# Second feed-forward network: 18 of 22 pairs of up tiles computed as seven products of blocks instead of eight

## The chip, the core and the metric

The kernel runs on one core of one Trainium2 chip. The metric is the device time of one execution, in microseconds (us). The engines that matter are TensorE (PE in the profile, with its weight loads as PEld), VectorE (DVE), ScalarE (ACT) and the DMA queue that SyncE issues (SPq). Each engine takes its instructions in its own order and waits for others by semaphores.

## The reference

A two-layer network steps 512 latent and 128 context tokens of width 1024. Layer 0 mixes tokens with a state-space scan, layer 1 with attention; behind each stands a gated feed-forward network with a convolution of width 3 over the tokens:

```
def conv_ffn(h, up_w, conv_w, conv_b, down_w):
    u = dwconv(h @ up_w, conv_w, conv_b)
    a, v = jnp.split(u, 2, axis=-1)
    return (jax.nn.silu(a) * v) @ down_w
```

`up_w` is 1024 x 5632, `down_w` 2816 x 1024, all in float32. The residual sum, gated, and a last norm follow. The other outputs (scan states, keys, values) are not touched by the change.

## The kernel before

**Layout.** All activations lie transposed: 8 feature tiles of 128 partitions by T = 640 tokens. A float32 operand is kept as a pair: a high part, rounded to the format that TensorE multiplies (`hi`, by ScalarE), and the rest (`lo = x - hi`, by VectorE). A product of two such operands is three matmuls: hi x hi, hi x lo, lo x hi.

**Weights** come in units of up to 128 x 1024 floats (512 KB). `prefetch` (L119) issues a unit's DMA into one of four `raw` buffers; `cast` (L127) splits it on ScalarE (`whi`, L95) and VectorE (`wlo`, L101); `nextw` (L140) keeps the loads three units and the split one unit ahead of TensorE.

**A feed-forward network** (`ffn`, L538) has 22 hidden tiles p (FT). Each needs a *pair* of up tiles: an `a` tile and a `v` tile of 128 features. `next_tile` (L314) runs `dense` over all 8 feature tiles of h: 8 steps x 3 matmuls, each cut into 256 and 384 columns (the halves A and B of the tokens) because a PSUM bank ends there; 48 matmuls a tile, 96 a pair. `copy_out` (L544) brings a tile from PSUM to SBUF on ScalarE. `epilogue` (L550) then does, for both tiles, the convolution (`conv`, L530: one ScalarE instruction and four on VectorE, of 511 and 127 columns), SiLU, the product and the split of the result into `mh` and `ml`, which are the moving operands of the down projection.

**Order.** `SUB` cuts the 22 hidden tiles into three groups, (0,8), (8,15) and (15,22). A stage of up pairs runs up to one pair past its group; then a down stage adds that group's share to all 8 output tiles (`project_out`, L275; for the last group `project_last`, L283, which also feeds the last norm). So the second network is: up 9 pairs, down 8 hidden tiles, up 7 pairs, down 7, up 6 pairs, down 7. Its first three up tiles come from `start_tiles` (L305), interleaved with the norm of h. The order in which each engine's instructions stand is fixed when the program is built: Python emits them in program order, and a scheduler of the framework may move them within an engine where dependencies allow.

**Places.** PSUM has three double banks (`dense_ps`, L115) for up and down tiles. The split weights have five buffers in the feed-forward networks (three in `pw`, two in `px`). Between the stages ScalarE and VectorE have much less to do than within the up stages.

Of the kernel before, what the change touches and what calls it, by code (L numbers as in the profile page):

```python
# [18 lines left out]
P = 128  # L19
D = 1024  # L20
KT = D // P
TP = 128
TS = 512
T = TP + TS
# [18 lines left out]
RSQRT_MAGIC = float(0x5F3759DF)  # L43


class Step:


    def __init__(self, ctx, tc, a):
        self.ctx, self.tc, self.nc, self.a = ctx, tc, tc.nc, a  # L50
        self.tasks = []
        self.ticks = 0
        self.wi = 0
        self.normt = {}
        self.ready = []
        self.px = None
        self.modtask = None
        self.late = []
        self.down = False
        self.wraw, self.wcast = {}, {}  # L60
        self.units = []
        pool = lambda n, b, **k: ctx.enter_context(tc.tile_pool(name=n, bufs=b, **k))
# [37 lines left out]
    def tt(self, out, a, b, op):  # L100
        return self.nc.vector.tensor_tensor(out, a, b, op)  # L101

    def mm(self, out, lhsT, rhs, start, stop):
        return self.nc.tensor.matmul(out, lhsT, rhs, start=start, stop=stop)  # L104

    def ct(self, shape, name, dt=F32):
        return self.pc.tile(shape, dt, tag=name, name=name)
# [11 lines left out]
    def prefetch(self, upto):  # L119
        while len(self.wraw) <= min(upto, len(self.units) - 1):  # L120
            u = len(self.wraw)
            ap, n = self.units[u]
            r = self.pw.tile([P, 1024], F32, tag="raw", name=f"raw{u}", bufs=RAW)
            self.nc.sync.dma_start(r[:, :n], ap)
            self.wraw[u] = r

    def cast(self, upto):  # L127
        while len(self.wcast) <= min(upto, len(self.units) - 1):
            u = len(self.wcast)
            self.prefetch(u)  # L130
            n = self.units[u][1]
            r = self.wraw[u]
            wp, t, b = (self.pw, "w", 3) if self.px is None or u % 5 < 3 else (self.px, "x", 2)
            hi = wp.tile([P, 1024], F32R, tag=t + "hi", name=f"whi{u}", bufs=b)
            lo = wp.tile([P, 1024], F32R, tag=t + "lo", name=f"wlo{u}", bufs=b)
            self.act(hi[:, :n], r[:, :n], AF.Copy)
            self.tt(lo[:, :n], r[:, :n], hi[:, :n].bitcast(F32), ALU.subtract)
            self.wcast[u] = (hi, lo)

    def nextw(self):  # L140
        u = self.wi
# [24 lines left out]
    def rsqrt(self, y, ms, n, count):  # L166
# [108 lines left out]
    def project_out(self, h, ks, g, tiles=range(KT)):  # L275

        for i in tiles:
            ps = self.dense_ps("po")
            self.dense(ps, self.nextw(), ks, h)
            for hf in "AB":  # L280
                self.gate_add(i, ps, g, hf)

    def project_last(self, h, ks, g, nextnorm, ks_last=None, parts="AB"):  # L283


        self.norm_begin()
        for i in range(KT - 3):
            ps = self.dense_ps("po")
            self.dense(ps, self.nextw(), ks, h)
            for hf in "AB":  # L290
                self.gate_add(i, ps, g, hf)
                self.norm_sq(i, hf)
        ks = ks_last or ks
        if self.modtask:
            self.drain(self.modtask)
        ws = [(self.dense_ps("po"), self.nextw(), i) for i in range(KT - 3, KT)]
        for hf in parts:
            for grp in ((ws[0:1], ws[1:3]) if hf == "B" else (ws[0:1], ws[1:2], ws[2:3])):
                self.dense_many([(ps, w, P) for ps, w, i in grp], ks, h, hf)
                for ps, w, i in grp:  # L300
                    self.gate_add(i, ps, g, hf)
                    self.norm_sq(i, hf)
            self.normt[hf] = self.add(nextnorm(hf), 3)
# [192 lines left out]
    def mod_rest(self, l, t0, pool):  # L496
# [41 lines left out]
    def ffn(self, l, h, nextnorm, pool):  # L538
        nc = self.nc
        cw = pool.tile([P, 2 * FT, 4], F32, tag="fcw", name=f"fcw{l}", bufs=1)  # L540
        nc.sync.dma_start(cw, self.a["fcw"][l])
        mid = {}

        def copy_out(ps):  # L544

            u = self.slot("f", "uraw", bufs=NF)
            self.act(u, ps[:, PO:PO + T], AF.Copy)
            return u

        def epilogue(p, ua, uv):  # L550
            ca = self.tmp("ca")
            self.conv(ca, ua, cw[:, p, :])
            cv = self.tmp("cv")
            self.conv(cv, uv, cw[:, FT + p, :])
            self.act(ca, ca, AF.Silu)
            self.tt(cv, ca, cv, ALU.mult)
            hi = self.slot("mh", f"mh{p}", F32R, bufs=9, pool=pool)
            lo = self.slot("ml", f"ml{p}", F32R, bufs=9, pool=pool)
# [10 lines left out]
        for s, (k0, k1) in enumerate(SUB):  # L569
            self.down = False  # L570
            while done < min(k1 + 1, FT):
                pair(done)
                done += 1
            self.down = True
            if s == len(SUB) - 1 and self.modtask:
                self.drain(self.modtask)
            if s < len(SUB) - 1:
                self.project_out(mid, range(k0, k1), self.gate(l, 1))
            else:
                self.project_last(mid, range(k0, k1), self.gate(l, 1), nextnorm, parts="CD" if l else "AB")  # L580


    def ssd_consts(self, pool):
# [505 lines left out]
    def attention(self, h, nextnorm, pool):  # L1089
# [5 lines left out]
        for hd in range(8):  # L1095
# [35 lines left out]
    def weight_units(self):  # L1131
        a = self.a
        u = [(a["w_dt"], 512)]
        xbc = lambda g: [16 + 4 * g + t for t in range(4)] + [32 + g, 36 + g]
        z = lambda g: [4 * g + t for t in range(4)]
        order = xbc(0) + xbc(1) + z(0) + xbc(2) + z(1) + xbc(3) + z(2) + z(3)
        u += [(a["w_in"][j], 1024) for j in order]
        for hf in range(2):
            u += [(a["w_so"][i, :, hf * 1024:(hf + 1) * 1024], 1024) for i in range(KT)]

        def ffn(l):
            done = 0
            out = []
            for k0, k1 in SUB:
                while done < min(k1 + 1, FT):
                    out.extend([(a["w_up"][l, done], 1024), (a["w_up"][l, FT + done], 1024)])
# [12 lines left out]
        return u  # L1159
# [131 lines left out]
```

## Time and profile before

| | us |
|---|---|
| median of three runs | 1894.25 |
| lowest and highest run | 1893.16, 1895.83 |
| span of the profiled execution | 1888.7 |
| PE, DVE, ACT busy in the span | 1855.0, 1366.3, 952.8 |

The profiled execution has no time of its own beside its span; the span runs from its first to its last instruction, and the median of the runs lies 5.5 us above it. The page's "busy" of an instruction runs from its start to its listed end, and successive instructions of one engine may overlap, so a sum of listed durations can exceed the busy time. In the rows of the timeline, the first two columns are the start and the length, both in us, and an x4 merges four instructions. In the chain of work that ended last, a row is a stretch in which one engine and one line carried the chain.

The second network lies at the end of the span. Its up and down stages can be read from the chain's rows `up` (up tiles) and `po` (down tiles).

### The profile page before, as it was taken

What the parts mean: (1) busy time and instruction counts of PE and PEld (TensorE: products, weight loads), DVE (VectorE), ACT (ScalarE), POOL (GpSimd) and SP (SyncE); (2) the same over time, 40 slices, a digit from 0 to 9 for tenths busy, and PEclk for the clock granted to TensorE, in tenths of its full rate; (3) what the DMA queues carried; (4) which work ended last, traced back from release to release, by engine and by line L of the source; (5) the groups of instructions that cost most, each with busy time, mean ns of one, the idle gap of its engine ahead of it and who ended that gap; (6) DMA issues with size and microseconds to landing.
All of it is one profiled execution on the core that took longest, in us unless ns stands there. A gap on an engine that the chain in (4) does not pass through costs nothing.

```text
span 1888.7 us, 32898 instructions
## 1 busy us (share of the span) xinstructions
PE 1855.0 (98%) x13333; PEld 1751.6 (93%) x13333; DVE 1366.3 (72%) x2640; ACT 952.8 (50%) x1748; POOL 0.2 (0%) x4
## 2 busy tenths in 40 slices
PE   7999999999999999999999999999999999999997
PEld 4799999989999999999999988888899999999996
DVE  4689999999758999974455877788686543553554
ACT  3479687878336441442443656566446432441441
POOL 0000000000000000000000000000000000000000
PEclk9999999999999999999999999999999999999998
DMA  9734243436533557632222211111132222222211
GB/s 346 261 108 139 97 145 107 133 123 197 186 107 124 189 173 227 190 102 80 75 70 71 74 57 57 60 48 38 36 124 79 79 74 73 74 72 79 73 40 56
DMA packets 79519, 209.71 MB, mean 111 GB/s; under 512 B 9116, under 2 KB 15880, under 8 KB 79240
## 3 DMA queue, kind: packets, MB, share of 16 engines
q1 hardware_dynamic: 78792, 207.10, 34.5%
q8 instruction: 104, 1.70, 0.4%
q10 hardware_dynamic: 576, 0.52, 0.1%
q14 instruction: 47, 0.39, 0.1%
HBM read 201.63 MB, written 5.96 MB: 110 GB/s over the span
## 4 chain that ended last, share of the span: by engine, by line
PE 93%; DVE 2%; ACT 2%; DMA 1%; issue 1%; SPq 0%; DVEq 0%; ACTq 0%
PE up L104 31%; PE po L104 25%; PE z L104 6%; PE x L104 5%; PE st L104 5%; PE v L104 3%; PE yp L104 3%; PE bc L104 2%; PE q L104 2%; PE sl L104 2%; PE k L104 2%; PE ov L104 2%; PE in L104 1%; PE wt L1065 1%; PE modrow L104 1%; ACT e L95 1%
## 5 line engine op out<-in xcount | busy, mean ns | idle before, releaser
L95 ACT ACTIVATE whi<-raw 128x1024 fp32r<-128x1024 f32 (+4 forms) x230 | 234.9, 1022 | 381.0 <-PE po L104 240.2
L101 DVE TENSOR_TENSOR wlo<-raw,whi 128x1024 fp32r<-128x1024 f32 (+4 forms) x230 | 270.2, 1175 | 176.2 <-ACT whi L95 164.7
L98 DVE SCALAR_TENSOR_TENSOR xr<-po,mod,xr 128x256 f32<-128x256 f32 (+2 forms) x231 | 88.8, 433 | 158.8 <-PE po L104 158.6
L104 PE MATMUL po<-mh,whi 128*128 128x256 f32 (+1 forms) x704 | 167.7, 310 | 0.0
L104 PE MATMUL po<-ml,whi 128*128 128x256 f32 (+1 forms) x704 | 167.5, 310 | 0.0
L104 PE MATMUL po<-mh,wlo 128*128 128x256 f32 (+1 forms) x704 | 167.3, 309 | 0.0
L104 PE MATMUL up<-h11h,wlo 128*128 128x256 f32 (+1 forms) x656 | 149.4, 309 | 0.0
L104 PE MATMUL up<-h01h,wlo 128*128 128x256 f32 (+1 forms) x656 | 149.4, 309 | 0.0
L104 PE MATMUL up<-h01l,whi 128*128 128x256 f32 (+1 forms) x656 | 149.3, 309 | 0.0
L104 PE MATMUL up<-h11h,whi 128*128 128x256 f32 (+1 forms) x656 | 149.3, 308 | 0.0
L104 PE MATMUL up<-h11l,whi 128*128 128x256 f32 (+1 forms) x656 | 149.3, 308 | 0.0
L104 PE MATMUL up<-h01h,whi 128*128 128x256 f32 (+1 forms) x656 | 149.3, 308 | 0.0
L104 PEld LDWEIGHTS po<-mh,whi 128*128 128x128 f32 x704 | 128.5, 188 | 0.6 <-ACT mh L95 0.4
L104 PEld LDWEIGHTS po<-mh,wlo 128*128 128x128 f32 x704 | 128.7, 188 | 0.0
L104 PEld LDWEIGHTS po<-ml,whi 128*128 128x128 f32 x704 | 128.6, 188 | 0.0
L104 PEld LDWEIGHTS up<-h01h,wlo 128*128 128x128 f32 x656 | 119.3, 188 | 0.0
L104 PEld LDWEIGHTS up<-h11h,whi 128*128 128x128 f32 x656 | 119.3, 188 | 0.0
L104 PEld LDWEIGHTS up<-h11h,wlo 128*128 128x128 f32 x656 | 119.3, 188 | 0.0
L104 PEld LDWEIGHTS up<-h11l,whi 128*128 128x128 f32 x656 | 119.3, 188 | 0.0
L104 PEld LDWEIGHTS up<-h01l,whi 128*128 128x128 f32 x656 | 119.3, 188 | 0.0
L104 PEld LDWEIGHTS up<-h01h,whi 128*128 128x128 f32 x656 | 119.3, 188 | 0.0
L95 ACT ACTIVATE mh<-cv 128x640 fp32r<-128x640 f32 x44 | 32.4, 737 | 121.3 <-DVE cv L101 121.3
(498 smaller groups left out, 4426.2 us busy)
## 6 DMA issues: line engine op xcount, KB each, us to landing
raw<-in_w_up SPq DMA_DIRECT2D x88, 512.0 KB, 3.5
mw<-in_modT SPq DMA_DIRECT2D x48, 512.0 KB, 4.3
raw<-in_w_in SPq DMA_DIRECT2D x40, 512.0 KB, 5.3
rb<-rowd SPq DMA_DIRECT2D x40, 512.0 KB, 5.3
raw<-in_w_dn SPq DMA_DIRECT2D x32, 448.0 KB, 3.3
raw<-in_w_qkv SPq DMA_DIRECT2D x24, 512.0 KB, 3.5
mr<-in_mod SPq DMA_DIRECT2D x44, 256.0 KB, 5.6
raw<-in_w_so SPq DMA_DIRECT2D x16, 512.0 KB, 4.2
```

The lines of the kernel that those rows point to most:

```text
L95: return self.nc.scalar.activation(out, in_, func, **k)
L98: return self.nc.vector.scalar_tensor_tensor(out, in0, s, in1, op0, op1)
L101: return self.nc.vector.tensor_tensor(out, a, b, op)
L104: return self.nc.tensor.matmul(out, lhsT, rhs, start=start, stop=stop)
L1065: nc.tensor.transpose(pm[:, b * P:(b + 1) * P], ws[b][:, kc * P:(kc + 1) * P], self.ident)
```

## The change

In the second network (l = 1), pairs 4 to 21 are no longer computed tile by tile. A pair is taken as a 2 x 2 block product: rows are the a tile and the v tile, the inner dimension is halved (feature tiles 0 to 3 and 4 to 7), and the columns are two halves of 320 tokens. The Winograd form of Strassen's scheme computes it with seven block products in place of eight.

- **Sums of h**, once: T1, T2, T4 (each for j = 0..3, 320 columns, split in hi and lo) and T3, which is written over a half of h that pairs 4 to 21 don't read any more. They are made during pairs 1 to 3 (`sums`, a task that moves on three `hook` steps at a time) and after pair 3 (`finish_sums`).
- **Sums of weights**, for each pair: s1 = y1+y2, s2 = s1-x1, s3 = x1-y1, s4 = x2-s2, where x and y are the raw a and v units and 1, 2 their halves of 512 columns; all on VectorE, in float32. Seven left operands of 512 columns (x1, x2, s2, s1, s3, s4, y2) are then split, against four halves (two whole units) before. The five split buffers hold two operands each. Splits run `LOOK` = 7 products ahead.
- **Products**: each is 4 steps x 3 matmuls of 320 columns; a pair is 84 matmuls. Four of the seven add onto another product in PSUM (bank `a`: 1, 6, 7, then 4; bank `c`: 5, then 3). ScalarE copies `a` out four times a pair (320 columns each), VectorE adds `b` or `c` to it three times. Products 3 and 4 of a pair run inside the next pair.
- **Between stages**: the last pair's products 3 and 4 and its epilogue come after the first down tile (`between`, i = 0); operands of the next stage are split during the later down tiles (i = 4 and 6), so that seven products are ready when it begins. `project_last` runs its first two tiles without their last inner step, which follows behind.
- `SUB` of this network is (0,7), (7,14), (14,22): up 8, down 7, up 7, down 7, up 7, down 8. `mh` and `ml` have 8 buffers instead of 9.

The core of the diff (new lines only, where not marked):

```
+STD = 4
+HT = T // 2
+LOOK = 7
-SUB = ((0, 8), (8, 15), (15, 22))
+SUB = (((0, 8), (8, 15), (15, 22)), ((0, 7), (7, 14), (14, 22)))
+MID = (9, 8)
...
+    def plan(self, p0, p1):
+        self.seq, self.done, self.at = [], 0, 0
+        for p in range(p0, p1):
+            prev = p > p0
+            self.seq += [(1, p), (2, p)] + [(3, p - 1)] * prev + [(6, p)] + [(4, p - 1)] * prev + [(5, p), (7, p)]
+        self.seq += [(0, p1 - 1), (3, p1 - 1), (4, p1 - 1)]
...
+                st.tt(s[0], y[:, k1], y[:, k2], ALU.add)
+                st.tt(s[1], s[0], x[:, k1], ALU.subtract)
+                st.tt(s[2], x[:, k1], y[:, k1], ALU.subtract)
...
+                st.tt(o["raw"][3], o["raw"][2], o["raw"][6], ALU.subtract)
+            if i not in o:
+                o[i] = self.place()
+                st.split_w(*o[i], o["raw"][i])
...
+    def product(self, ps, i, p):
+        st = self.st
+        self.at += 1
+        self.stage(self.at + LOOK)
+        wh, wl = self.ops[p].pop(i)
+        acc = i in (6, 7, 3, 4)
+        for j in range(4):
+            xh, xl = self.t[self.B[i], j]
+            c = slice(j * P, j * P + P)
+            for m, (a, b) in enumerate(((wh, xh), (wh, xl), (wl, xh))):
+                st.mm(ps, a[:, c], b, not acc and j == 0 and m == 0, j == 3 and m == 2, skip_group_check=acc)
+            st.hook()
...
+    def pair(self, p):
...
+        self.product(a, 1, p)
+        st.act(ua[:, c1], a, AF.Copy)
+        self.product(b, 2, p)
+        st.tt(ua[:, c1], ua[:, c1], b, ALU.add)
+        if self.pend:
+            self.third()
+        self.product(a, 6, p)
+        st.act(ua[:, c2], a, AF.Copy)
+        if self.pend:
+            self.fourth()
+        self.product(c, 5, p)
+        self.product(a, 7, p)
+        st.act(uv[:, c2], a, AF.Copy)
+        st.tt(uv[:, c2], uv[:, c2], c, ALU.add)
+        self.pend = p, a, c, ua, uv
+
+    def third(self):
+        p, a, c, ua, uv = self.pend
+        self.product(c, 3, p)
+        self.st.tt(ua[:, HT:], ua[:, HT:], c, ALU.add)
+
+    def fourth(self):
+        p, a, c, ua, uv = self.pend
+        self.product(a, 4, p)
+        self.st.act(uv[:, :HT], a, AF.Copy)
+        self.epilogue(p, ua, uv)
+        self.pend = None
...
     while done < end:
-                pair(done)
+                if l and done >= STD:
+                    blk.pair(done)
+                else:
+                    pair(done)
+                    if l and done == 0:
+                        sums = self.add(blk.sums(), 2)
+                    if l and done == STD - 1:
+                        self.drain(sums)
+                        blk.finish_sums()
```

**Where instructions stand now.** VectorE in the middle of an up stage, before: one pair, in which `wlo` are the low halves of a whole weight unit, `ca` and `cv` the convolutions of the two tiles and `ml` the low half of the result.

```order
2105 L101 TENSOR_TENSOR wlo_16859<-raw_16724,whi_16858 128x1024
2106 L98 SCALAR_TENSOR_TENSOR ca<-uraw,fcw_15575,ca 128x511
2107 L98 SCALAR_TENSOR_TENSOR ca<-uraw,fcw_15575,ca 128x127
2108 L98 SCALAR_TENSOR_TENSOR ca<-uraw,fcw_15575,ca 128x511
2109 L98 SCALAR_TENSOR_TENSOR ca<-uraw,fcw_15575,ca 128x127
2110 L101 TENSOR_TENSOR wlo_16917<-raw_16781,whi_16916 128x1024
2111 L98 SCALAR_TENSOR_TENSOR cv<-uraw,fcw_15575,cv 128x511
2112 L98 SCALAR_TENSOR_TENSOR cv<-uraw,fcw_15575,cv 128x127
2113 L98 SCALAR_TENSOR_TENSOR cv<-uraw,fcw_15575,cv 128x511
2114 L98 SCALAR_TENSOR_TENSOR cv<-uraw,fcw_15575,cv 128x127
2115 L101 TENSOR_TENSOR cv<-ca,cv 128x640
2116 L101 TENSOR_TENSOR ml_16720<-cv,mh_16719 128x640
```

VectorE in the second up stage now: what stands from pair 10's `uv` sum (which product 3 of that pair waits for) to that pair's convolutions, `s` being the weight sums, `bb`, `bc` and `ba` PSUM.

```order
2291 L283 TENSOR_TENSOR uv_17543<-uv_17543,bb 128x320
2292 L283 TENSOR_TENSOR s_12_17688<-raw_17683 128x512
2293 L283 TENSOR_TENSOR ml_17646<-cv,mh_17645 128x640
2294 L283 TENSOR_TENSOR s_12_17689<-s_12_17688,raw_17681 128x512
2295 L283 TENSOR_TENSOR s_12_17690<-raw_17681,raw_17683 128x512
2296 L283 TENSOR_TENSOR wlo_17696<-raw_17681,whi_17695 128x1024
2297 L283 TENSOR_TENSOR ua_17686<-ua_17686,bc 128x320
2298 L283 TENSOR_TENSOR wlo_17726<-s_11_17547,whi_17725 128x512
2299 L283 TENSOR_TENSOR wlo_17726<-s_12_17689,whi_17725 128x512
2300 L283 TENSOR_TENSOR ua_17542<-ua_17542,bb 128x320
2301 L283 TENSOR_TENSOR s_12_17691<-raw_17681,s_12_17689 128x512
2302 L283 TENSOR_TENSOR wlo_17759<-raw_17538,whi_17758 128x512
```

The sums and splits of the next pairs and the sums out of PSUM have moved in between the pieces of the epilogue; the epilogue itself is the same.

VectorE where the block products begin (pair 4): the end of the sums of h (`ht` and the low halves `T_3`) and pair 3's convolutions stand ahead of `wlo_16277`, the low half of pair 4's first operand.

```order
2088 L283 TENSOR_TENSOR T_3_16210<-hs,T_3_16210 128x320
2089 L283 TENSOR_TENSOR ht<-hr,hs 128x320
2090 L283 TENSOR_TENSOR T_3_16213<-hs,T_3_16213 128x320
2091 L283 TENSOR_TENSOR s_4_16271<-raw_16019,raw_16114 128x512
2092 L283 TENSOR_TENSOR T_3_16216<-ht,T_3_16216 128x320
2093 L280 SCALAR_TENSOR_TENSOR ca<-uraw,fcw_15575,ca 128x511
2094 L280 SCALAR_TENSOR_TENSOR ca<-uraw,fcw_15575,ca 128x127
2095 L280 SCALAR_TENSOR_TENSOR ca<-uraw,fcw_15575,ca 128x511
2096 L280 SCALAR_TENSOR_TENSOR ca<-uraw,fcw_15575,ca 128x127
2097 L283 TENSOR_TENSOR wlo_16277<-raw_16019,whi_16276 128x1024
```

All of the sums of h, the epilogues of pairs 0 to 2 and part of pair 3's have been put ahead of the first block product's operand.

TensorE within an up stage before: one step of one tile, three matmuls in two pieces each.

```order
9241 L104 MATMUL up<-h11h_15420,whi_16726 128x256
9242 L104 MATMUL up<-h11h_15420,whi_16726 128x384
9243 L104 MATMUL up<-h11l_15421,whi_16726 128x256
9244 L104 MATMUL up<-h11l_15421,whi_16726 128x384
9245 L104 MATMUL up<-h11h_15420,wlo_16727 128x256
9246 L104 MATMUL up<-h11h_15420,wlo_16727 128x384
```

TensorE in the second up stage now: the end of product 6 of pair 12 (`ba`), the last matmul of product 4 of pair 11 (`bb<-T_3_16216`), product 5 of pair 12 (`bb`, operand `wlo_17759`) and the first of its product 7 (`ba<-h11h`); an x2 merges a matmul by the high and one by the low half of T.

```order
9719 L286 MATMUL ba<-T_3_16213,whi_17725 128x320 x2
9720 L286 MATMUL ba<-T_3_16213,wlo_17726 128x320
9721 L286 MATMUL bb<-T_3_16216,wlo_17759 128x320
9722 L286 MATMUL bb<-T_0_15922,whi_17758 128x320 x2
9723 L286 MATMUL bb<-T_0_15922,wlo_17759 128x320
9724 L286 MATMUL bb<-T_1_16031,whi_17758 128x320 x2
9725 L286 MATMUL bb<-T_1_16031,wlo_17759 128x320
9726 L286 MATMUL bb<-T_2_16132,whi_17758 128x320 x2
9727 L286 MATMUL bb<-T_2_16132,wlo_17759 128x320
9728 L286 MATMUL bb<-T_3_16210,whi_17758 128x320 x2
9729 L286 MATMUL bb<-T_3_16210,wlo_17759 128x320
9730 L286 MATMUL ba<-h11h_15408,whi_17807 128x320
```

Where 256 and 384 columns of one tile alternated over 48 matmuls, runs of about twelve matmuls of 320 columns go into different PSUM tiles in turn.

More of the change, by code (lines that the diff above doesn't have):

```diff
@@ L101, in tt, with mm @@
         return self.nc.vector.tensor_tensor(out, a, b, op)
[L103 to L104 removed]
+    def mm(self, out, lhsT, rhs, start, stop, **k):
+        return self.nc.tensor.matmul(out, lhsT, rhs, start=start, stop=stop, **k)
     def ct(self, shape, name, dt=F32):
@@ L130, in cast, with parts, split_w @@
             self.prefetch(u)
+            if u in self.paired:
+                self.wcast[u] = None
+                continue
             n = self.units[u][1]
[L132 to L138, printed above, removed]
+            hi, lo = (t[:, :n] for t in self.parts())
+            self.split_w(hi, lo, self.wraw[u][:, :n])
+            self.wcast[u] = hi, lo
+    def parts(self):
+        v = self.npart
+        self.npart += 1
+        wp, t, b = (self.pw, "w", 3) if self.px is None or v % 5 < 3 else (self.px, "x", 2)
+        return [wp.tile([P, 1024], F32R, tag=t + nm, name=f"w{nm}{v}", bufs=b) for nm in ("hi", "lo")]
+    def split_w(self, hi, lo, raw):
+        self.act(hi, raw, AF.Copy)
+        self.tt(lo, raw, hi.bitcast(F32), ALU.subtract)
     def nextw(self):
@@ L273, in gate_add, with project_out @@
             self.stt(self.x[i][:, a:b], ps[:, COL0[half] + a:COL0[half] + b], g[:, i, c:c + 1], self.x[i][:, a:b], ALU.mult, ALU.add)
-    def project_out(self, h, ks, g, tiles=range(KT)):
+    def project_out(self, h, ks, g, tiles=range(KT), after=None):
         for i in tiles:
@@ L568, in ffn @@
         done = 0
-        for s, (k0, k1) in enumerate(SUB):
+        sub = SUB[l]
+        blk = Blocks(self, h, epilogue, pool) if l else None
+        for s, (k0, k1) in enumerate(sub):
+            last = s == len(sub) - 1
             self.down = False
-            while done < min(k1 + 1, FT):
-                pair(done)
+            end = min(k1 + 1, FT)
+            if blk and s == 0:
+                blk.plan(STD, end)
+            while done < end:
+                if l and done >= STD:
+                    blk.pair(done)
+                else:
+                    pair(done)
[4 more added lines that the diff above has]
+                        blk.finish_sums()
                 done += 1
             self.down = True
-            if s == len(SUB) - 1 and self.modtask:
+            if last and self.modtask:
                 self.drain(self.modtask)
-            if s < len(SUB) - 1:
-                self.project_out(mid, range(k0, k1), self.gate(l, 1))
-            else:
-                self.project_last(mid, range(k0, k1), self.gate(l, 1), nextnorm, parts="CD" if l else "AB")
+            after = blk and (lambda i: blk.between(i, done, min(sub[s + 1][1] + 1, FT) if not last else done))
+            if not last:
+                self.project_out(mid, range(k0, k1), self.gate(l, 1), after=after)
+            else:
+                self.project_last(mid, range(k0, k1), self.gate(l, 1), nextnorm, parts="CD" if l else "AB",
+                                  after=after)
     def ssd_consts(self, pool):
@@ L1143, in ffn @@
             out = []
-            for k0, k1 in SUB:
+            for k0, k1 in SUB[l]:
                 while done < min(k1 + 1, FT):
+                    if l and done >= STD:
+                        self.paired |= {len(u) + len(out), len(u) + len(out) + 1}
                     out.extend([(a["w_up"][l, done], 1024), (a["w_up"][l, FT + done], 1024)])
```

130 lines of the change are left out of this document (125 added, 5 removed).

## The prediction

> **What bounds the kernel now.** I read the page first (busy time, the chain that ended last), then the chain in order of time over the second network, then its stages in windows, then single rows for prices.
>
> ```profile
> span 1888.7 us, 32898 instructions
> PE 1855.0 (98%) x13333; PEld 1751.6 (93%) x13333; DVE 1366.3 (72%) x2640; ACT 952.8 (50%) x1748; POOL 0.2 (0%) x4
> PE 93%; DVE 2%; ACT 2%; DMA 1%; issue 1%; SPq 0%; DVEq 0%; ACTq 0%
> ```
>
> TensorE carries 93% of the chain. The span is 5.5 us shorter than the median of 1894.25; I take changes as differences and add them to the median. In the chain the second network's stages read:
>
> ```profile
> 1426.48 105.61 PE up L104 x720
> 1532.09 56.31 PE po L104 x384
> 1588.40 98.63 PE up L104 x672
> 1687.03 49.80 PE po L104 x336
> 1736.83 84.53 PE up L104 x576
> ```
>
> Each up stage is matmuls without a break: 105.61 / 720 = 0.1467 us each, 7.04 us a tile of 48, 14.08 us a pair of 96. Nothing else is on the path there. How much the others have in hand, by windows (columns: PE, PEld, DVE, ACT):
>
> ```profile
> 600.00:650.00 50.00, 50.00 (x343) 50.00 (x342) 49.93 (x84) 23.15 (x29) 0.00 (x0) 1.00 0.55 174
> 650.00:700.00 50.00, 50.00 (x343) 50.00 (x342) 49.90 (x89) 22.59 (x28) 0.00 (x0) 1.00 0.57 181
> 1426.00:1532.00 106.00, 106.00 (x724) 106.00 (x723) 65.00 (x100) 53.81 (x66) 0.00 (x0) 1.00 0.27 85
> 1532.00:1581.00 49.00, 49.00 (x335) 49.00 (x334) 18.40 (x31) 9.52 (x10) 0.00 (x0) 1.00 0.24 76
> ```
>
> In the first up stage VectorE is busy 65 of 106 us, in the down stage behind it 18.4 of 49. The first network (600 to 700) shows that VectorE can be busy 99.8% of the time with TensorE at its full 343 matmuls per 50 us.
>
> **The change part by part.** *TensorE.* What 320 columns cost stands in no row, so it is bounded by 256 and 384:
>
> ```profile
> 1480.01 0.28 PE L104 MATMUL up<-h11h,whi 128*128 128x256 f32 x1
> 1480.13 0.34 PE L104 MATMUL up<-h11h,whi 128*128 128x384 f32 x1
> 1480.31 0.28 PE L104 MATMUL up<-h11l,whi 128*128 128x256 f32 x1
> ```
>
> From start to start 256 columns take 0.12 us and 384 take 0.18: time follows columns, 0.2934 us for 640, so I take half of that, 0.147 us, between the ends 0.12 and 0.18. A pair is then 84 x 0.1467 = 12.32 us, 1.76 less; eighteen pairs save **31.7 us** if nothing but TensorE counts. The down tiles keep their matmuls (7+7+8 hidden tiles instead of 8+7+7).
>
> *VectorE.* Its listed durations overlap, so prices are differences of starts in rows that follow each other without idle:
>
> ```profile
> 1426.01 1.94 DVE L98 SCALAR_TENSOR_TENSOR ca<-uraw,fcw,ca 128x511 f32<-128x511 f32 x4 [0.77 <-ACT ca L95]
> 1427.87 1.93 DVE L98 SCALAR_TENSOR_TENSOR cv<-uraw,fcw,cv 128x511 f32<-128x511 f32 x4
> 1429.71 1.22 DVE L101 TENSOR_TENSOR wlo<-raw,whi 128x1024 fp32r<-128x1024 f32 x1
> 1430.85 0.82 DVE L101 TENSOR_TENSOR cv<-ca,cv 128x640 f32<-128x640 f32 x1
> 1431.59 1.67 DVE L98 SCALAR_TENSOR_TENSOR ca<-uraw,fcw,ca 128x511 f32<-128x511 f32 x3
> ```
>
> ```profile
> 300.18 0.68 DVE L101 TENSOR_TENSOR qc<-qc,bc 128x512 f32<-128x512 f32 x1
> 300.79 0.31 DVE L98 SCALAR_TENSOR_TENSOR rs_a<-rs_y 128x160 f32<-128x160 f32 x1
> 303.86 0.68 DVE L101 TENSOR_TENSOR h<-h,st 128x512 f32<-128x512 f32 x1
> 304.46 0.32 DVE L98 SCALAR_TENSOR_TENSOR rs_a<-rs_a 128x160 f32<-128x160 f32 x1
> ```
>
> ```profile
> 78.41 0.48 DVE L98 SCALAR_TENSOR_TENSOR spp<-spp,spu 128x320 f32<-128x320 f32 x1
> 78.81 0.34 DVE L98 SCALAR_TENSOR_TENSOR cacc<-x,scw,cacc 128x127 f32<-128x127 f32 x1
> ```
>
> Four convolution instructions cost 1.86, a split of 1024 columns 1.14, 640 columns 0.74, 512 columns 0.61 (0.60 with an operand, `st`, in PSUM), 320 columns 0.40. A pair before: 2 x 1.86 + 2 x 0.74 + 2 x 1.14 = 7.48 us. A pair after: the epilogue's 5.20; four weight sums, 4 x 0.61 = 2.44; seven low halves, 4.27 (4.19 where x is split whole); three sums out of PSUM, 1.20. That is **13.1 us**, against 12.32 on TensorE: in the steady state VectorE, not TensorE, has the longer list, by 0.75 us a pair, still 1 us under the 14.08 of before. ScalarE gets three casts of 512 columns more and four copies of 320 for two of 640; at 53.8 of 106 us it has room.
>
> The same rows put in doubt a rule that speaks against the change. By the Trainium skill, VectorE: DVE Perf Modes, section Terms, a flush follows every instruction and the next can't issue until the pipe is empty; the rows disagree, since `cv<-ca,cv` starts 1.14 us after a split that lists 1.22.
>
> *First up stage* (pairs 0 to 7). The sums of h come on top, while pairs 1 to 3 still run the old way. VectorE has these instructions from the start of pair 0's convolutions (1426.0) up to the sum `uv` of pair 6, in its order: epilogues of pairs 0 to 4 (26.0) and pair 5's but for its last split (4.5); two old splits (2.3); eight sums of h over 640 columns, 28 sums and splits of 320 (17.1); four splits of T3 (1.6); 16 weight sums (9.8), 2 splits of 1024 and 22 of 512 (15.7); seven sums out of PSUM (2.8): 79.8 us, to 1505.8 at the earliest. From there TensorE has products 3, 6, 4, 5, 7, 8.8 us, to 1514.6; products 3 and 4 of pair 7, which have moved into the down stage, make it 1518.1. Before, pair 7 ends 13 tiles behind 1426.48, at 1518.0. So the 7.0 us that four pairs would save are gone, with VectorE never idle; I add 2 us for its waits: **9.0 lost**. Part of it shows where pair 4 begins: its first operand's `wlo` has 40 of these us ahead of it and comes at 1466, while TensorE is done with pair 3 at 1426.48 + 5 x 7.04 = 1461.7. What a stop does to the clock is bounded by
>
> ```profile
> 1300.00:1350.00 50.00, 48.15 (x308) 41.83 (x307) 41.93 (x82) 32.13 (x65) 0.00 (x0) 0.97 0.10 29
> ```
>
> 0.03 x 50 = 1.5 us for one dip, and nothing if none comes; I take 1.5. Beside it: the Trainium skill, TensorE: Matmul & The Clock Gate, Part 1, has the clock halved after an idle window of 3.4 us until TensorE has been busy as long; by it a stop of 4.3 us costs about 1.7 us.
>
> *Second and third up stage* (seven pairs each). Seven products are split ahead, in a down stage where VectorE has 30 us free. TensorE alone would take 7 x 12.32 = 86.2 instead of 98.63. The lead lasts about two pairs; the other five run at VectorE's 13.07: 5 x 0.75 = 3.75 lost a stage, **7.5** for both. The lead may also hide all of it (0).
>
> *Waits that are new on TensorE*: product 6 for ScalarE's copy of product 1, with product 2 (1.76 us) between, against a copy of at most 0.6 us (640 columns, below): nothing, while ScalarE isn't blocked. Product 3 for VectorE's `uv` sum, with products 1 and 2 of the next pair (3.5 us) between; behind it TensorE's whole queue stands. That is where VectorE's longer list will show. The second down tile takes PSUM that the copy of product 4 has to leave: copy plus passing on, 0.7 us, three times, 2.1; at the end pair 21's epilogue starts a product later against the same cover: 0.8.
>
> ```profile
> 1511.68 0.69 ACT L95 ACTIVATE uraw<-up 128x640 f32<-128x640 f32 x1
> raw<-in_w_up SPq DMA_DIRECT2D x88, 512.0 KB, 3.5
> ```
>
> *DMAs* keep their number and order. A raw buffer is held longer: in VectorE's order a pair's first weight sum comes 1.6 to 6.8 us behind the last reader of the buffer that it loads into, and a load takes 3.5. That can stop VectorE for some 2 us near the start of a stage, where it waits for TensorE anyway: nothing. Eight `mh` buffers for groups of 7 and 8: nothing, since the next result comes after the down stage.
>
> **Sum:** -31.7 + 9.0 + 1.5 + 7.5 + 2.1 + 0.8 = -10.8; 1894.25 - 10.8 = **1883.5 us**.
>
> **The rivals.** *The lead hides VectorE's excess.* Then the later stages lose nothing and the first 7: -31.7 + 7 + 1.5 + 2.1 + 0.8 = -20.3, 1874 us. For it: VectorE at 99.8% in the first network. Against: there the filling was independent; here each low half follows a ScalarE instruction.
>
> *VectorE's waits for ScalarE, in order, become the bound: slower.* Before, every pair has one wait for `mh` and two for the convolutions:
>
> ```profile
> DVE ml L101 <- ACT mh L95: 3.2, 4, 0.8
> DVE ca L98 <- ACT ca L95: 1.3, 4, 0.3
> DVE cv L98 <- ACT cv L95: 1.0, 3, 0.3
> ```
>
> 0.8 + 0.3 + 0.3 = 1.4 us, harmless there. If the new instructions between don't cover them, or ScalarE, itself waiting for a product to copy, holds back a cast behind it, thirteen pairs (three in the first stage, five in each later one) run 1.4 us longer: +18.2, and 1883.5 + 18.2 = 1902 us. It decides from 10.8 / 13 = 0.83 us a pair. For it: every piece of an epilogue now waits for a product and a copy just before it. Against: at every such place the order has sums or splits of the next pair in front.
>
> *About 0.5 to 1 us a pair is lost so*: within 0.2% of before (a measurement of this kernel can't tell less from no change), about 1894.
>
> *VectorE takes its listed durations in full*, a mechanism of this kernel's rows:
>
> ```profile
> L98 DVE SCALAR_TENSOR_TENSOR ca<-uraw,fcw,ca 128x511 f32<-128x511 f32 x16 | 12.0, 747 | 2.3 <-ACT ca L95 2.3
> L98 DVE SCALAR_TENSOR_TENSOR ca<-uraw,fcw,ca 128x127 f32<-128x127 f32 x16 | 5.5, 344 | 0.0
> ```
>
> 0.75 x 4 + 0.34 x 4 + 0.82 x 2 + 11 x 0.68 + 3 x 0.48 = 14.9 us a pair, 2.6 over TensorE: ten pairs 26, the first stage 79.8 x 14.9 / 13.1 = 90.8, so 18 + 2 lost: -31.7 + 20 + 1.5 + 26 + 2.9 = +18.7, 1913 us. It is the flush rule named above; the starts speak against it.
>
> That the products aren't fewer can be left out: 84 matmuls a pair stand in the order.
>
> **How the numbers follow.** Forecast, 1877 to 1890: 0.52. Lead hides it, below 1877: 0.15. Level, 1890.5 to 1898: 0.12. Waits for ScalarE: 0.18. Full durations: 0.03. So faster 0.67, same 0.12, slower 0.21. The range, 1872 to 1903, leaves out the full durations, the far side of the waits and the case in which the first stage loses little.
>
> **What would show it.** Right: matmuls of 320 columns 0.147 us apart; VectorE over 95% busy from 1430 to the end of the first up stage and in the later part of the others; a stop of TensorE of some 4 us before the first block product, released by `wlo`; up stages of seven pairs of 84 to 88 us. Wrong: VectorE with more than 1 us of waits for ScalarE in each pair, TensorE waiting for `uv` sums or copies by more than 1 us a pair, or 320 columns nearer to 0.18 us.

## The result and the profile after

| | before | after |
|---|---|---|
| median of four runs, us | 1894.24 | 1882.38 |
| lowest and highest | 1893.16, 1895.83 | 1879.61, 1884.19 |
| ratio, 95% interval | | 0.9933 (0.9917 to 0.995) |
| span of the profiled execution | 1888.7 | 1882.4 (its own time 1884.19) |

The change makes the kernel 12 us faster, 0.7%, with an interval that lies clear of 1; 1883.5 was forecast. The page of after:

```profile
span 1882.4 us, 32863 instructions
PE 1841.4 (98%) x13117; PEld 1727.3 (92%) x13117; DVE 1478.4 (79%) x2886; ACT 991.6 (53%) x1880; POOL 0.2 (0%) x4
```

216 matmuls fewer, 216 x 0.1467 = 31.7 us, and 112 us more of VectorE; two thirds of TensorE's gain are gone again. To see where, I compare the executions in place. The first matmul of an up tile stands at 1426.3 us in before and at 1430.3 in after; ahead of it nothing is changed, and over the runs below this point scatters from 1428.4 to 1432.3. From there to the end: 462.4 us before, 452.1 after, **10.3 us less**. The three up stages of after in windows (length; busy time and instructions of PE, PEld, DVE, ACT, POOL; the clock granted to TensorE; DMA share and GB/s), with a piece of the first:

```profile
1430.34:1527.20 96.86, 89.11 (x555) 85.79 (x555) 88.12 (x164) 56.52 (x94) 0.00 (x0) 0.93 0.22 67
1465.50:1496.00 30.50, 23.22 (x112) 20.70 (x111) 23.93 (x43) 10.29 (x20) 0.00 (x0) 0.78 0.16 52
1580.37:1665.88 85.51, 84.90 (x566) 82.66 (x565) 77.49 (x139) 52.92 (x90) 0.00 (x0) 1.00 0.26 78
1719.19:1804.72 85.53, 84.92 (x565) 82.70 (x565) 77.48 (x139) 52.91 (x90) 0.00 (x0) 1.00 0.25 81
```

The first stage issues 552 matmuls, and two of the first down tile's stand ahead of its last product (the window counts those on its edges too). At 0.1467 us the 554 are 81.3; it takes 96.9, so **15.6 are lost** (15.9 where the expectations below leave the two out). Of these 14 lie in the 30 us behind the first block product, where TensorE is stopped or at half clock and VectorE, too, is idle for 6.6 us. The other two stages issue 564, 82.7 us, and take 85.5: 2.8 lost each. The chain of work that ended last shows the down stage between them (start, length, count):

```profile
1527.36 5.86 PE po L286 x40
1533.22 1.76 PE bc L286 x12
1534.98 1.76 PE bb L286 x12
1536.74 43.79 PE po L286 x294
```

The two products that moved behind the first down tile (`bc`, `bb`) run at full rate, and the second down tile follows without a stop.

What stops the first stage stands in the timeline behind pair 3 (start, length, instruction; in brackets the idle time before it and who ended it):

```profile
1467.02 0.31 PE L286 MATMUL bc<-h11l,whi 128*128 128x320 f32 x1
1469.17 0.42 PE L286 MATMUL ba<-h11h,wlo 128*128 128x320 f32 x1 [1.84 <-DVE wlo L283]
...
1470.42 0.47 PE L286 MATMUL ba<-h11l,whi 128*128 128x320 f32 x1
1470.69 0.47 PE L286 MATMUL ba<-h11h,wlo 128*128 128x320 f32 x1
...
1472.48 0.63 PE L286 MATMUL ba<-h11h,whi 128*128 128x320 f32 x1 [0.53 <-ACT ua L277]
...
1479.53 0.31 PE L286 MATMUL bc<-h11h,wlo 128*128 128x320 f32 x1
...
1481.38 0.48 DVE L283 TENSOR_TENSOR ua<-ua,ba 128x320 f32<-128x320 f32 x1
1481.91 0.56 PE L286 MATMUL ba<-T,whi 128*128 128x320 f32 x2 [2.07 <-DVE ua L283]
...
1484.27 1.06 ACT L277 ACTIVATE whi<-raw 128x1024 fp32r<-128x1024 f32 x1 [6.76 <-PE ba L286]
1485.23 0.42 ACT L277 ACTIVATE ua<-ba 128x320 f32<-128x320 f32 x1
1485.70 0.64 PE L286 MATMUL ba<-h11h,whi 128*128 128x320 f32 x1 [1.20 <-ACT ua L277]
```

The forecast stop is there (1469.17, for the first low half): 3.6 us behind the first block matmul at 1465.56, with only six matmuls in them, where some 4 us were forecast. Others weren't forecast, three of them shown. At 1472.48 product 2 waits for ScalarE's copy of product 1; at 1481.91 product 6 waits for VectorE's sum of product 2, which stands behind splits in VectorE's list; at 1485.70 product 7 waits for a copy that stands behind a split in ScalarE's list, and that split had itself waited 6.76 us for TensorE. Behind the first stop matmuls are 0.27 us apart instead of 0.147 (1470.42, 1470.69): half clock (0.27 is not twice 0.147, but the granted clock is 0.50 from 1470 to 1475). In the piece from 1465.5 the clock is 0.78, so (1 - 0.78) x 30.5 x 2 = 13 us of it ran at half.

The waits of products 2 and 6 can be seen in the instruction order. Both are for the *other half* of the double bank `ba`: a is its first half, b its second. In brackets stands whom the instruction waits for (`Activation` is ScalarE).

```
9210 L286 MATMUL ba_16314<-h11h4_15416,whi170_16276 128x320 [waits Activation_49]
9239 L286 MATMUL ba_16314<-T2_0_15925,whi171_16281 128x320 [waits DVE_49]
```

Product 2 writes b and waits for the reader of a; product 6 adds onto a and waits for the reader of b. The order keeps dependences by tile, and the tile is the double bank.

### The profile page after: what moved, and what is told of

It reads as the page before. It is cut to its first block, busy times and chain, and to the rows that moved or that the text cites. A ratio compares the mean times of both kernels' runs of the same rounds, so it can differ in the third digit from the quotient of the medians.

```text
span 1882.4 us, 32863 instructions
## 1 busy us (share of the span) xinstructions
PE 1841.4 (98%) x13117; PEld 1727.3 (92%) x13117; DVE 1478.4 (79%) x2886; ACT 991.6 (53%) x1880; POOL 0.2 (0%) x4
## 5 line engine op out<-in xcount | busy, mean ns | idle before, releaser
L277 ACT ACTIVATE whi<-raw 128x1024 fp32r<-128x1024 f32 (+4 forms) x238 | 228.3, 961 | 303.1 <-PE po L286 187.7
L283 DVE TENSOR_TENSOR wlo<-raw,whi 128x1024 fp32r<-128x1024 f32 (+4 forms) x238 | 261.9, 1102 | 79.7 <-ACT whi L277 67.8
L277 ACT ACTIVATE whi<-s 128x512 fp32r<-128x512 f32 x72 | 44.5, 626 | 60.7 <-PE po L286 20.6
L277 ACT ACTIVATE e<-sl,sm 128x640 f32<-128x640 f32 x64 | 50.4, 790 | 40.2 <-DVE sm L1225 39.8
L286 PE MATMUL z<-h00h,whi 128*128 128x256 f32 (+1 forms) x256 | 62.9, 325 | 0.0
L277 ACT ACTIVATE e<-rb,Ctok 128x128 f32<-128x128 f32 x160 | 56.4, 390 | 12.3 <-issue 10.0
L277 ACT ACTIVATE ca<-ca 128x640 f32<-128x640 f32 x44 | 32.4, 736 | 57.0 <-DVE ca L280 56.8
L286 PE MATMUL z<-h00l,whi 128*128 128x256 f32 (+1 forms) x256 | 59.8, 312 | 0.0
```

What stands on the lines that cost most here:

```text
L277: return self.nc.scalar.activation(out, in_, func, **k)
```

## The experiments

**Theory:** the first stage loses because VectorE's added work doesn't fit into the time before and behind pair 4. **Rivals:** the order in which ScalarE and VectorE serve the first products (then it is lost wherever these begin), and half clock. For the later stages: VectorE's rate (13.1 us a pair against 12.32), as forecast, or something else.

### Where the products begin: pair 6 and pair 8

```
-STD = 4
+STD = 6
```

> Block products begin with pair 6 instead of pair 4. Lengths are of the first up stage in place, from its first matmul of an up tile to the first one of the down tile behind it; after it was 96.9 us, of which 15.4 stops and half clock. Theory (VectorE's amount of work, spread over too short a stage): two pairs of 13.1 us become pairs of 7.5, 11 us less, and TensorE has 3.5 us more to do, 84.5 alone in place; 2 to 4 us lost, 87 to 89 us, time about 1874. Rival (the order of ScalarE and VectorE behind TensorE's first products costs this wherever they begin): 15 us lost, 100 us, time about 1886. Second rival (half clock is the whole matter, one stop is enough for it): 5 to 8 us lost, 91 us, about 1877.

For pair 8 (`STD = 8`) nothing is pending at the first down tile, so the plan begins there:

```
-            if blk and s == 0:
-                blk.plan(STD, end)
...
+            if self.pend:
+                self.third()
+                self.fourth()
```

> Block products only in the second and third group of pairs, 8 to 21; the first group runs as before, with the sums of h beside it. Theory (amount of work in too short a stage): the first up stage has 13 tiles of 7.04 us, 91.5, with no stop; the second and third up stage as after, 85.5 us each; time about 1873.5. Rival (starting the products costs it wherever they begin): 10 to 15 us of stops and half clock move to the head of the second up stage, which then takes 97 us, time about 1886.

Measured: from pair 6 1873.71 us, ratio 0.9878 (0.9861 to 0.9894); from pair 8 1876.60, 0.9893 (0.9879 to 0.9908). First and second up stage, of the run from pair 6 and then of that from pair 8:

```profile
1431.66:1517.52 85.86, 85.33 (x577) 84.50 (x577) 76.96 (x139) 52.50 (x81) 0.00 (x0) 1.00 0.24 76
1570.95:1656.49 85.54, 84.93 (x565) 82.70 (x565) 77.48 (x139) 52.91 (x90) 0.00 (x0) 1.00 0.26 78
```

```profile
1429.12:1520.65 91.53, 91.53 (x625) 91.53 (x625) 72.80 (x127) 52.48 (x74) 0.00 (x0) 1.00 0.27 81
1569.63:1655.17 85.54, 84.93 (x565) 82.71 (x565) 77.50 (x139) 52.91 (x90) 0.00 (x0) 1.00 0.26 78
```

With two pairs fewer in blocks the loss falls from 15.6 to 1.4 us (85.9 against 84.5 alone, less even than the 2 to 4 that the theory gave); with none it is zero, and the second stage, where the products then begin, doesn't take it over: 85.5 as in after. Starting them costs nothing by itself; starting them while VectorE still sums does. Pair 8 is slower than pair 6 because two pairs fewer run in blocks: 3.5 us of TensorE's time against the 1.4 lost; the medians are 2.9 us apart, and the runs of each scatter by 2 to 4 us.

### Less and more work for VectorE

Without the sums of h the products read halves of h:

```
+            for i, k, c in ((1, j, c2), (2, j + 4, c2), (4, j + 4, c1)):
+                self.t[i, j] = self.h[k][0][:, c], self.h[k][1][:, c]
```

> Leaves out the sums of h and their splits (the products read halves of h itself): 8 sums of 640 columns, 16 of 320 and 16 low halves of 320 off VectorE, 5.9 + 6.4 + 6.4 = 18.7 us, and 16 high halves off ScalarE. Theory (amount): VectorE is through before pair 4 is due, no stop of over 1 us and no half clock, first up stage 82 to 85 us in place (81 alone) against 96.9; the later up stages unchanged at 85.5. Rival (order behind the first products): the stops behind the first product stay, 91 us or more.

Without the sums of weights:

```
+                o["raw"] = {1: x[:, k1], 2: x[:, k2], 4: y[:, k2], 5: y[:, k1], 6: y[:, k2], 7: y[:, k1], 3: y[:, k1]}
```

> Leaves out the sums of weights (the operands are halves of the raw units): four of 0.61 us a pair off VectorE, 13.1 to 10.7 us a pair, less than TensorE's 12.32. Theory: in the later up stages only the stop of 0.8 us near the end goes, since the lead already hides the rest, 84.7 us against 85.5, and steps of 0.1 us at some 19 products stay; the first up stage gets 6 to 9 us shorter, 88 to 91. Rival (VectorE's rate sets the later stages): both become 83 us or less. Second rival (order, not amount, in the first stage): it stays at 95 or more.

With each of these made twice:

```
+                for n, v, w, f in ((0, y[:, k1], y[:, k2], ALU.add), (1, s[0], x[:, k1], ALU.subtract),
+                                   (2, x[:, k1], y[:, k1], ALU.subtract)):
+                    st.tt(s[n], v, w, f)
```

> Each of the four sums of weights of a pair is made twice: 4 x 0.61 = 2.4 us a pair more on VectorE, 15.5 us against TensorE's 12.32; nothing else changes. Theory (a stage is paid by VectorE's total between its own lead and its own tail, not by its rate): VectorE was busy 77.5 of the 85.5 us of a later up stage; 7 x 2.4 = 17 us more make 92 to 95 with a lead of one pair done before, so the later up stages become 91 to 97 us; the first one 103 to 108 in place. Rival (the lead hides about any excess of VectorE): 85.5 to 87. Second rival (VectorE's rate sets the pace as soon as it is above TensorE's): 7 x 15.5 = 108 less one pair's lead, 100 or more.

First up stage without the sums of h (a single run, 1867.87 us); first and second without the sums of weights (1876.26); and with these twice (1907.11):

```profile
1428.44:1512.67 84.23, 82.94 (x555) 81.29 (x555) 71.04 (x125) 49.27 (x78) 0.00 (x0) 1.00 0.25 77
```

```profile
1430.00:1518.57 88.57, 82.85 (x553) 80.96 (x553) 78.42 (x146) 56.17 (x94) 0.00 (x0) 1.00 0.24 74
1572.03:1657.55 85.52, 85.07 (x565) 82.74 (x565) 66.66 (x119) 52.47 (x90) 0.00 (x0) 1.00 0.26 78
```

```profile
1432.31:1534.03 101.72, 90.64 (x567) 87.08 (x567) 97.58 (x180) 56.96 (x94) 0.00 (x0) 0.93 0.20 64
1585.61:1680.00 94.39, 87.58 (x565) 82.75 (x565) 88.55 (x160) 53.63 (x90) 0.00 (x0) 1.00 0.22 72
```

The first stage follows VectorE's amount: 84.2, 88.6 and 101.7 us against 96.9, the last one less than the 103 to 108 of its theory. Leaving out the sums of h also takes 7 us off ScalarE (56.5 to 49.3); leaving out the sums of weights takes none (56.2), and there the stage gets 8.3 us shorter, so that this part is VectorE's. In the second, 11 us less of VectorE (77.5 to 66.7 busy) change nothing, 85.5 still, so the 2.8 us lost there aren't VectorE's; that was wrong in the theory's 84.7 as well. Doubling makes it 94.4, within the forecast 91 to 97 and far from the 100 that a rate of 15.5 us a pair would give. So VectorE's excess isn't paid pair by pair, and nothing is paid while its total fits beside TensorE's time. That the total alone sets the length once it doesn't fit is not shown: VectorE is busy 88.6 of the 94.4 us and idle for 5.8, and of the 17 us added only 11 lie in the stage.

### Half clock by itself

```
+        if p == STD:
+            for n in range(22):
+                st.mm(a, self.ops[p][1][0][:, :P], self.t["11", 0][0], True, True, skip_group_check=True)
         self.product(a, 1, p)
```

> Ahead of pair 4's first product 22 matmuls of 320 columns are added, 3.2 us, which product 1 overwrites; they need only the high half that is there when TensorE stops, so they lie in the stop of some 3 us before the first low half. Theory (the half clock behind the stop costs by itself): the first stretch of half clock goes, 24 matmuls by 0.12 us, 2.9 us, and perhaps the second, 2 us more; first up stage 92 to 94.5 us in place against 96.9 though TensorE does more. Rival (VectorE and ScalarE pace this stretch, half clock or not): 96 to 98. Second rival (the products wait behind the added matmuls): 99 or more.

```profile
1432.13:1526.76 94.63, 87.14 (x578) 84.51 (x577) 87.94 (x164) 56.84 (x94) 0.00 (x0) 1.00 0.22 69
```

The clock is 1.00, and the stage takes 2.2 us less with 3.2 us more of matmuls in it. The added matmuls lie in the stop; half clock had cost about 2.2 us, near the forecast (92 to 94.5) but not where the theory put it. From the stage's start, product 6 begins after 51.6 us in the changed kernel and 51.4 here, so the first stretch of half clock cost next to nothing: TensorE then waits for VectorE anyway. The gain comes behind it, where the second stretch had been. TensorE stopped here, too, for 2.9 us and 2.4 us start to start (at 1479.69 and 1483.50), without half clock:

```profile
1479.69 0.42 PE L289 MATMUL bc<-h11h,wlo 128*128 128x320 f32 x1 [2.62 <-DVE wlo L286]
1483.50 0.57 PE L289 MATMUL ba<-T,whi 128*128 128x320 f32 x2 [2.07 <-DVE ua L286]
```

In the whole execution (1884.30, a single run) the gain can't be seen.

### Two results in one double bank

The exchange puts b into the double bank that the next pair's b shares, and c beside a:

```
-            return x[:, :HT], x[:, 512:512 + HT], y[:, :HT]
+            return x[:, :HT], y[:, :HT], x[:, 512:512 + HT]
...
-        return y[:, 512:512 + HT], z[:, :HT], z[:, 512:512 + HT]
+        return z[:, :HT], y[:, 512:512 + HT], z[:, 512:512 + HT]
```

With products from pair 6:

> As the run from pair 6, but the results b and c change places in PSUM: a and c share a double bank, b has a half of another. Theory (a product waits for reads of its own double bank, of the other half too: product 2 for the copy of product 1, product 6 for VectorE's sum of product 2): with a and b apart these waits go, the steps of 0.25 us at some 19 products a stage fall to under 10 and the later up stages from 85.5 to 83.5 to 84.8 us; time 1870 to 1873. Rival (the steps belong to every wait, whatever bank): 85.5 us, time 1873.7. Second rival (a and c together, product 5 now waits for the copy behind product 6): 86.5 or more.

Measured: 1869.05 us, 0.9861 (0.9846 to 0.9875). The theory holds: the second up stage takes 83.8, three matmuls of the down tile (0.4 us) among them, which leaves 0.6 of the 2.8 us lost, and the late steps in it (a matmul that starts at least 0.03 us later behind the one before than the columns of that take) go from 24 to 6. The edit is these lines alone, but the scheduler then puts ScalarE's and VectorE's instructions in another order, too; what that adds to the gain isn't separated. First and second up stage:

```profile
1431.20:1515.88 84.68, 84.68 (x578) 84.48 (x578) 77.17 (x139) 52.73 (x81) 0.00 (x0) 1.00 0.26 77
1569.05:1652.81 83.76, 83.70 (x568) 83.03 (x568) 77.61 (x140) 53.60 (x90) 0.00 (x0) 1.00 0.27 84
```

With products from pair 4, the exchange is the only edit to the changed kernel:

> The changed kernel with b and c exchanged in PSUM and nothing else (products from pair 4). Theory (VectorE's amount makes the first stage's loss, the shared double bank only adds to it): of 15.9 us lost in the first up stage 2 to 5 go, 92 to 95 us in place against 96.9; the later up stages 83.8 us each; time 1874 to 1878. Rival (the waits for the other half of a double bank are the main cause there): 83 to 88 us, time 1866 to 1871.

Measured: 1872.24, 0.9888 (0.987 to 0.9906). The first up stage falls from 96.9 to 89.2, further than the theory's 92 to 95 and not as far as the rival's 83 to 88; both causes are real. The window has four matmuls of the down tile (0.6 us), so 7.7 us are still lost:

```profile
1428.90:1518.15 89.25, 84.00 (x557) 81.53 (x557) 86.71 (x161) 57.23 (x94) 0.00 (x0) 1.00 0.23 73
```

In the order, the first matmul of product 6 now waits for ScalarE alone:

```
9220 L286 MATMUL ba_16314<-T2_0_15925,whi171_16281 128x320 [waits Activation_49]
```

What is left with the exchange is tested by taking the sums of h out as well (left out as above):

> Products from pair 4, b and c exchanged, and the sums of h with their splits left out (the products read halves of h itself), 18.7 us off VectorE. Theory (what the exchange left of the first stage's loss, 8.3 us, is VectorE's amount of work): first up stage 81 to 82 us in place, 81 alone, against 89.2. Rival (a part belongs to the order behind the first products whatever VectorE has to do): 83.5 us or more, some 2.5 us or more of stops left.

A single run, 1865.35 us:

```profile
1431.67:1512.84 81.17, 81.17 (x554) 80.97 (x553) 70.82 (x123) 49.93 (x78) 0.00 (x0) 1.00 0.26 81
```

That closes the account of the first stage. Lost beside TensorE's time for the matmuls in the window: 15.6 with both causes, 7.7 with the amount of work alone, 3.0 with the shared bank alone, 0.2 with neither. (The amount is VectorE's and, for the sums of h, some of ScalarE's.) Together the two cause 4.9 more than one by one; half clock, which only the run with both of these four shows (0.93 against 1.00), is 2.2 of that by the added matmuls, and the rest I can't divide.

### Between the two: pair 5

> Block products begin with pair 5. Theory (amount): one pair of 13.1 us on VectorE becomes one of 7.5, so against the run from pair 4 the backlog falls by 5.6 us and TensorE has 1.76 more to do, 82.7 alone in place; stops 4 to 8 us, with at most one stretch of half clock, 87 to 91 us; time 1874 to 1878, between the runs from pair 4 and from pair 6. Rival (all is lost at the first product, as soon as VectorE is behind by one pair): 95 us, time 1882.

> Products from pair 5, b and c exchanged. Theory: 90.0 us of the first up stage become 86 to 88.5, later ones 83.8; time 1871 to 1874, above the run from pair 6. Rival: 83 to 85 us, time 1867 to 1869, as good as from pair 6 or better.

Measured without the exchange: 1878.26, 0.9916 (0.9899 to 0.9933), first stage 90.0, 7.3 of it lost. With it: **1866.80, 0.9858 (0.9842 to 0.9873)**, the lowest median here of a version of which no part is left out (its interval overlaps that of the run from pair 6). Its first up stage and the two later ones:

```profile
1429.52:1512.31 82.79, 82.79 (x566) 82.70 (x566) 81.75 (x152) 54.83 (x87) 0.00 (x0) 1.00 0.24 74
1565.50:1648.95 83.45, 83.45 (x569) 83.05 (x568) 77.68 (x140) 53.30 (x90) 0.00 (x0) 1.00 0.27 85
1701.72:1786.30 84.58, 84.25 (x569) 83.22 (x569) 77.81 (x140) 53.70 (x90) 0.00 (x0) 1.00 0.28 88
```

Here the rival won against my theory: VectorE is busy 81.75 of 82.79 us and TensorE loses nothing (82.7 alone). All 7.3 us of the run without the exchange go with it: the shared bank's waits turn a VectorE that is just keeping up into stops. Of the later stages the second loses 0.3 us and the third 1.3.

### The sums of h on GpSimd

```
-            st.tt(t1, a[:, c2], a[:, c1], ALU.subtract)
+            g.tensor_tensor(t1, a[:, c2], a[:, c1], ALU.subtract)
```

and so for all 24.

> Products from pair 4, b and c exchanged, and the 24 sums of h (8 of 640 columns, 16 of 320, 5.9 + 6.4 = 12.3 us on VectorE) on GpSimd, which has nothing else to do; the splits stay. No run so far shows how long GpSimd takes for them. Theory (amount on VectorE): 12.3 us less before pair 4, the first up stage 6 to 9 us shorter than with the exchange alone, 84 to 88 us; time 1868 to 1871. Rival (GpSimd takes so long, or slows VectorE so much, that T2 and T4 come late): no shorter than with the exchange alone, 92 us or more.

Measured: 1884.58, 0.995 (0.9933 to 0.9967); the rival. The window of the first up stage, then groups of equal instructions from 1428.57 to 1470 (busy us, mean ns), of this run and, in the third block of lines, of the run with the exchange alone:

```profile
1428.57:1529.30 100.73, 85.66 (x553) 84.88 (x553) 90.71 (x139) 56.33 (x94) 32.10 (x21) 0.90 0.21 65
```

```profile
L71 POOL TENSOR_TENSOR hr<-h11h,h11l 128x640 f32<-128x640 f32 x6 | 12.7, 2131 | 3.0 <-DVE T L283 3.0
L283 DVE TENSOR_TENSOR T<-hs,T 128x320 fp32r<-128x320 f32 x6 | 5.0, 831 | 4.4 <-ACT T L277 4.4
L280 DVE SCALAR_TENSOR_TENSOR ca<-uraw,fcw,ca 128x127 f32<-128x127 f32 x6 | 4.7, 779 | 0.0
```

```profile
L283 DVE TENSOR_TENSOR T<-hs,T 128x320 fp32r<-128x320 f32 x8 | 3.7, 482 | 0.0
L280 DVE SCALAR_TENSOR_TENSOR ca<-uraw,fcw,ca 128x127 f32<-128x127 f32 x8 | 2.7, 342 | 0.0
```

GpSimd takes 2.1 us on average for a sum of 640 columns (VectorE 0.82), and VectorE's own instructions get longer beside it: 482 to 831 ns, 342 to 779. VectorE has 22 instructions fewer in the stage and is busy 4 us longer. Most of the 19.8 us lost (100.7 against 81.0) is one stop of TensorE:

```profile
1476.19 0.47 ACT L277 ACTIVATE T<-hs 128x320 fp32r<-128x320 f32 x1 [0.93 <-POOL hs L80]
1476.57 0.69 ACT L277 ACTIVATE uraw<-up 128x640 f32<-128x640 f32 x1
1477.31 0.64 PE L286 MATMUL bb<-h11h,whi 128*128 128x320 f32 x1 [11.48 <-ACT uraw L277]
```

ScalarE's copy of an up tile of pair 3, for which TensorE waits, stands behind ScalarE's splits of the last sums of h, and these wait for GpSimd. How much of the delay is GpSimd's own time and how much VectorE's longer instructions isn't separated.

## Why the prediction was right, step by step

The time came out within 1.2 us, and the first cause was right, but the closeness is partly luck: the first up stage cost 5 us more than forecast, and the other losses together nearly 5 us less.

| term | forecast, us | measured in place, us |
|---|---|---|
| TensorE, 18 pairs x 1.76 | -31.7 | -31.7 (216 matmuls) |
| first up stage, with the clock | +9.0 + 1.5 | +15.6 |
| second and third up stage | +7.5 | +5.5 |
| second down tile, three times | +2.1 | +0.7 (first two down stages) |
| tail | +0.8 | -0.4 (from the last down stage on) |
| sum | -10.8 | -10.3 |

- **First up stage.** VectorE's backlog was sized nearly right: 9.0 forecast, 7.7 where the shared bank is out of the way, with ScalarE's share in it not separated. The step that failed is "product 6 for ScalarE's copy of product 1 ...: nothing". Product 6 waits for VectorE's sum of product 2, because b lies in the same double bank, and product 2 for the copy of product 1. It shows wherever VectorE is late: with the exchange, which takes this wait away, the stage gets 7.6 us shorter. The wait stood in the order, as a wait for VectorE on product 6's first matmul; I had taken the waits from the data alone. "VectorE never idle" fell with it: busy 88.1 of 96.9 us.
- **Half clock.** 1.5 forecast, 2.2 measured, but not from the forecast stop: what half clock cost came behind a stop that wasn't forecast. Beside it the Trainium skill, TensorE: Matmul & The Clock Gate, Part 1, which has the clock halved after an idle window of 3.4 us: here the stop ahead of the second stretch was 2.4 us (1479.53 to 1481.91). Nor is a stop of that size sure to do it: the run with the added matmuls stopped TensorE for 2.9 and 2.4 us, the one without the sums of weights for 2.0 and 2.5, and both kept 1.00. A rule by the longest single stop doesn't decide here.
- **Later up stages.** The step "the lead lasts about two pairs; the other five run at VectorE's 13.07" failed; the rival that the lead hides VectorE's excess was right on it. VectorE's busy 77.5 of 85.5 us has room, because the splits of the next seven products are made in the down stage before and the last epilogue in the one behind. What was lost is mostly waits on shared banks (2.2 of the 2.8 in the second stage go with the exchange in the run from pair 6). The stages came out at 85.5, inside the 84 to 88 that I had named as the sign of VectorE's rate: a sign that another cause can give too.
- **Waits of VectorE for ScalarE** were the slower rival. They exist in a later stage,

```profile
DVE wlo L283 <- ACT whi L277: 3.1, 2, 2.7
...
DVE ca L280 <- ACT ca L277: 1.3, 2, 1.0
...
DVE uv L283 <- ACT uv L277: 0.4, 1, 0.4
DVE cv L280 <- ACT cv L277: 0.3, 2, 0.2
```

  5.1 us in seven pairs, 0.7 a pair, and no cost of them shows, VectorE having 8 us free.
- **Full durations on VectorE** (14.9 us a pair) is out: in the stage of 82.79 us of the run from pair 5 with the exchange, the listed durations of VectorE's instructions add up to 94 us, and TensorE doesn't stop.
- **Second down tile**: the copy of product 4 never stopped TensorE; 0.15 us from its last matmul to the down tile's next.

## What to carry to other kernels

Where the order of instructions keeps dependences by tile, two results in one tile wait for each other's readers: put together what is read at the same time, and read the waits on the first matmul of each product before costing it at nothing. New work for an engine beside the bound one costs nothing while its total in a stage, lead and tail included, fits; start what depends on it when it does, here one pair later. And name as a sign of a cause only what the other causes would not give as well.

## What was not expected of the hardware

- GpSimd beside VectorE: with GpSimd's elementwise sums under way, 32 us in all, two kinds of VectorE's instructions took 1.7 and 2.3 times as long (831 ns against 482, 779 against 342). The Trainium skill, SBUF — State Buffer, "Who interferes with whom", says that a VectorE instruction with two SBUF inputs contends with a GpSimd instruction that reads SBUF; the trace agrees.
- TensorE can do more in less time: 22 useless matmuls in a stop kept the clock up and shortened the stage by 2.2 us.
